# Four sample pages a run in the heads' stage, and the decay levels of the gated linear attention in two runs a head

## The chip, the cores and the metric

The kernel runs on 1 core of one Trainium2 chip. The metric is the device time of one launch in microseconds (us), as the median of three runs; the kernel before takes 1266.97 us (1264.0 to 1270.75).

## The reference, cut to what matters

One inference step of a decoder layer with two parallel head groups. 512 prompt tokens and 8 sequences of 8 sample tokens go through one input projection; eight heads do sparse attention over the 256 (128 for the prompt) best keys of an indexer, four heads do gated linear attention (GLA); both are gated and go through one output projection. The two parts that the change touches:

```python
# sample tokens: attention over 8 cache pages of 128 keys per sequence, with a mask from the indexer's top 256
s = einsum('bthd,btkhd->bthk', q, k_sel) * DH_A ** -0.5
p = softmax(where(valid, s, NEG_BIG))
out = einsum('bthk,btkhd->bthd', p, v_sel)

# GLA, inside a chunk: every pair t >= s is weighted by the decay between s and t
diff = cum[t] - cum[s]
att = einsum('bhtk,bhsk,bhtsk->bhts', qt, kt, exp(where(causal, diff, -inf)))
o = o_inter + einsum('bhts,bhsv->bhtv', att, vt)
S_new = exp(last) * S + einsum('bhsk,bhsv->bhkv', kt * exp(last - cum), vt)
```

## The kernel before

All of the 576 tokens stand as columns, in two fp32r halves (xh, xl). The projection is cut into 65 blocks of 128 output columns; `gemm` does a block in two halves, each with one weight piece (`wload`: w_raw by DMA on SP's queue, w_hi on ACT, w_lo on DVE or POOL, three buffers of each) and 48 matmuls of 288 columns (L218). These matmuls are what TensorE does most of the time. Stages follow each other: the indexer's blocks, the sample tokens' index scores (`sample_scores`, over cache pages), eight attention heads, four GLA heads, gates, output projection.

Work on the sample tokens is cut into pieces by generators and put between the weight pieces: `gemm` calls `fill` after each half, and a rate (R0, R1, RF) says how many pieces a half brings. `unit(un, w, hg)` is the attention of four sequences (w) and four heads (hg). For each half of the keys it takes the four sequences' pages (kt, 1 MB for each, as four 256 KB DMAs with page numbers read on SP), and the same over eight pages of values (vt). Its matmuls have 32 stationary columns, and four of them, for four heads, stand at the four column groups of the array (`tile_position=(0, 32 * g)`). They come in runs of two pages: `run` issues the first matmul where it is ready and holds the others right behind it, so that a run is 8 matmuls without a gemm matmul between. Two page buffers (`tag="kv", bufs=2`) serve a run. Two units run in the heads' stage (heads 4 to 7), two in the GLA stage.

In a GLA head, the decay between two tokens is built by levels B = 64, 32, 16, 8, 4, 2, 1 and the diagonal (B = 0). For each level POOL makes differences of the cumulated log decay (L879, L880), ACT the exponential (L881), DVE the products with k and q (L882, L883) into a buffer `lv_d` (two of them). Then TensorE multiplies 32 by 32 blocks into the PSUM tile `pl`: the two coarse levels in one run, every other level in a run of its own, in the order column group outside, token block i inside (L250 is a run's first matmul, L253 the others). A coarse level is copied to `att` by ACT, the others are copied under a mask `lm` to `attD` by DVE (L907, L909).

TensorE executes an fp32 matmul as two passes, so each stands twice in the trace. The order of all instructions is set by a scheduler that simulates the program; each engine, and SP's queue of DMA issues, then goes through its list in order. `page_dma` holds a page's load behind the third page before it. PSUM has three banks that rotate (`mm1`, tag "pm") and one of its own for the units (tag "pu").

Of the kernel before, what the change touches and what calls it, by code (L numbers as in the profile page):

```python
# [70 lines left out]
def shape_constants():  # L71
# [37 lines left out]
    )  # L109
    s_, t_ = i[:, None] % 32, i[None, :32]  # L110
    lm = []
    for b in LEVELS[2:]:
        lm.append((s_ // (2 * b) == t_ // (2 * b)) & (s_ % (2 * b) < b) & (t_ % (2 * b) >= b))
    lm.append(s_ == t_)
    lm = np.stack(lm, 1).astype(np.float32)
    return {k: np.ascontiguousarray(v, dtype=np.float32) for k, v in parts.items()}, lm


def build(tc, I, O):
# [3 lines left out]
    WOFF = 400  # L123
    R0, R1, RF = 0.7, 0.8, 2

# [165 lines left out]
    po_.tensor_copy(selw, sel32)  # L291
    lm = cp.tile([P, 6, 32], U8, name="lm")
    lm32 = p0.tile([P, 6, 32], F32, name="lm32")
    sy.dma_start(lm32, I["k_lm"])
# [398 lines left out]

    def unit(un, w, hg):
        qz = ev.tile([P, 4, 4, 32], F32, name="qz", tag="e0", bufs=2)
# [49 lines left out]
        pO = pm.tile([P, 512], F32, name="pOs", tag="pu", bufs=1)  # L745
        for j0 in range(0, NPAGE, 2):
            mms = []
            for j in (j0, j0 + 1):
                vt = un.tile([P, 4, 512], F32, name="vt", tag="kv", bufs=2)
                page_dma(  # L750
                    lambda bb: vt[:, bb, :], lambda r: I["cv"][r, :, 512 * hg : 512 * hg + 512].rearrange("o s c -> (o s) c"),
                    NB * NPAGE + 4 * (NPAGE * w + j), 4,
                )
                mms[:0] = [
                    partial(
                        pe.matmul, pO[32 * g : 32 * g + 32].rearrange("p (b d) -> p b d", b=4), prT[:, j, 32 * g : 32 * g + 32],
                        vt[:, :, P * g : P * (g + 1)], start=(j == 1), stop=False, tile_position=(0, 32 * g),
                    )
                    for g in range(4)
                ]  # L760
            if j0 == NPAGE - 2:
                mms += [
# [48 lines left out]

    us = chain(unit(un, 0, 1), unit(un, 1, 1))
    filler[:] = [us, R1, 0.0]
# [8 lines left out]

    wg = gl.tile([P, TP], F32, name="wg", tag="lv_d", bufs=2)
    sy.dma_start(wg[64:], I["w_gate_up"])
    wgh = gl.tile([P, TP], F32R, name="wgh", tag="lv_d", bufs=2)
    se.copy(wgh[64:], wg[64:])
# [13 lines left out]
    def log_decay(h):  # L840
        e_ = gl.tile([P, T], F32, name="ld_e", tag="lv_d", bufs=2)
        mn = gl.tile([P, T], F32, name="ld_m", tag="lv_d", bufs=2)
        for j in range(2):
# [13 lines left out]
    for h in range(HB):  # L857
# [12 lines left out]
        po_.memset(attD, 0.0)  # L870
        coarse = []
        for lv, B in enumerate(LEVELS + (0,)):
            n = T if B <= 4 else TP
            if B:
                d = gl.tile([P, T], F32, name="lv_d", tag="lv_d", bufs=2)
                half = lambda x: x[:, :n].rearrange("p (m two b) -> p m two b", two=2, b=B)
# [6 lines left out]
                ve.tensor_tensor(out=dv[:, :, 1, :], in0=dv[:, :, 1, :], in1=half(qT)[:, :, 1, :], op=ALU.mult)  # L883
                kd, qd = d, d
            else:
                kd, qd = kT, qT
            pl = mm1("pl")
            if B >= 32:
                coarse[:0] = [
                    partial(  # L890
                        pe.matmul, pl[r0 + u : r0 + u + 32, B * i : B * i + B], kd[:, P * i + r0 + u : P * i + r0 + u + 32],
                        qd[:, P * i + r0 + B : P * i + r0 + 2 * B], start=True, stop=True, tile_position=(0, r0 + u),
                    )
                    for i in range(4) for r0 in range(0, P, 2 * B) for u in range(0, B, 32)
                ]
                if B == 32:
                    run(*coarse)
                    for pl_, b_ in ((pl64, 64), (pl, 32)):
                        for r0 in range(0, P, 2 * b_):
                            se.copy(att[r0 : r0 + b_, :, r0 + b_ : r0 + 2 * b_], pl_[r0 : r0 + b_, : 4 * b_].rearrange("p (i t) -> p i t", i=4))  # L900
# [7 lines left out]
            if n == T:  # L908
                ve.copy_predicated(attD[:TS, 4, :], lm[:TS, lv - 2, :], pl[:TS, P : P + 32])  # L909
        for g in range(4):  # L910
# [14 lines left out]
        ve.tensor_mul(qE, qT, eC)  # L925
        kD = gl.tile([P, T], F32, name="kD", tag="lv_d", bufs=2)
        po_.tensor_tensor(out=kD[:, :TP].rearrange("p (i t) -> p i t", t=P), in0=cP[:, :, P - 1 : P].to_broadcast([P, 4, P]), in1=cP, op=ALU.subtract)
# [309 lines left out]
```

## Time and profile before

| | us |
|---|---|
| median of 3 runs | 1266.97 |
| lowest and highest | 1264.0, 1270.75 |
| the profiled execution | 1268.29 |
| its span on the core | 1266.5 |
| TensorE busy (98% of the span) | 1244.3 |
| DVE, ACT, POOL busy | 645.7, 540.0, 248.1 |

The profile comes from one execution. Its engines' busy times are unions of instructions in flight, so that a busy TensorE can still lose time where one kind of matmul gives way to another; the timeline, with the start of each group of matmuls, shows that. The granted TensorE clock is 0.996 of 2.4 GHz over the span. The index scores of the sample tokens lie at 145 to 212 us, heads 4 to 7 with the first two units at 382 to 648 us, and the GLA heads at 648 to 980 us.

### The profile page before, as it was taken

Reading aid. Unit: us, or ns where it says so; the run is one execution under the profiler, and the core shown is the slowest. Engines: PE = TensorE matmul, PEld = TensorE weight load, DVE = VectorE, ACT = ScalarE, POOL = GpSimd, SP = SyncE. Lnnn points to the kernel's source line nnn. Section 1 sums busy time; section 2 is a strip of 40 time slices with the busy share of each in tenths; the row PEclk is TensorE's granted clock in tenths of the full one; section 3 lists DMA queues with packets and bytes.
Section 4 is the critical chain, followed back from the end, with each engine's and each line's share of the span. In section 5 each row is a group of like instructions: output and inputs, shape, how many; then the busy total and the mean of one; then the engine's idle time right before and its main releaser. Section 6 shows DMA issues by size and latency. Waiting matters only on the chain.

```text
span 1266.5 us, 24037 instructions
## 1 busy us (share of the span) xinstructions
PE 1244.3 (98%) x9419; PEld 1133.1 (89%) x9419; DVE 645.7 (51%) x1204; ACT 540.0 (43%) x917; POOL 248.1 (20%) x307
## 2 busy tenths in 40 slices
PE   9999999999999999999999999999999999999997
PEld 8999988999998988888988888888999998888896
DVE  6677999999544334342444444444544533323233
ACT  6966775243333423242343633545444432222233
POOL 0224433343501010000104113022120210102021
PEclk9999999999999999999999999999999999999998
DMA  9642132223426566657457585574513634333335
GB/s 322 230 142 84 59 104 84 91 66 105 156 93 230 196 226 209 231 203 229 153 179 250 169 274 198 188 247 155 157 52 121 208 103 133 102 102 121 89 104 166
DMA packets 94852, 200.39 MB, mean 158 GB/s; under 512 B 11394, under 2 KB 28051, under 8 KB 94035
## 3 DMA queue, kind: packets, MB, share of 16 engines
q1 hardware_dynamic: 93650, 197.41, 47.6%
q8 instruction: 74, 1.21, 0.4%
q10 hardware_dynamic: 1088, 1.45, 0.4%
q14 instruction: 40, 0.32, 0.1%
HBM read 179.93 MB, written 18.76 MB: 157 GB/s over the span
## 4 chain that ended last, share of the span: by engine, by line
PE 80%; DVE 7%; DMA 6%; SPq 3%; ACT 2%; issue 2%; DVEq 0%; ACTq 0%
PE ps_g L218 46%; PE ps_g L226 5%; PE acc L1102 4%; PE acc L1104 4%; PE acc L1103 4%; SPq L156 2%; DVE wk L494 2%; DMA kt<-in_ck 2%; PE pOs L253 1%; PE pl L253 1%; PE pS L250 1%; PE pOs L250 1%; DMA xr<-in_xT 1%; DMA vt<-in_cv 1%; PE pS L253 1%
## 5 line engine op out<-in xcount | busy, mean ns | idle before, releaser
L218 PE MATMUL ps_g<-xh,w_hi 128*128 128x288 f32 x1824 | 402.8, 299 | 0.0
L218 PE MATMUL ps_g<-xl,w_hi 128*128 128x288 f32 x1824 | 401.7, 298 | 0.0
L218 PE MATMUL ps_g<-xh,w_lo 128*128 128x288 f32 x1824 | 398.7, 297 | 0.0
L180 ACT CAST w_hi<-w_raw 128x1024 fp32r<-128x1024 f32 x158 | 165.7, 1049 | 379.3 <-PE ps_g L218 209.2
L218 PEld LDWEIGHTS ps_g<-xh,w_hi 128*128 128x128 f32 x1824 | 296.5, 189 | 12.1 <-issue 9.2
L218 PEld LDWEIGHTS ps_g<-xh,w_lo 128*128 128x128 f32 x1824 | 296.1, 189 | 7.8 <-issue 6.3
L218 PEld LDWEIGHTS ps_g<-xl,w_hi 128*128 128x128 f32 x1824 | 296.3, 189 | 5.4 <-issue 3.7
L182 DVE TENSOR_TENSOR w_lo<-w_raw,w_hi 128x1024 fp32r<-128x1024 f32 x126 | 155.8, 1237 | 239.6 <-ACT w_hi L180 224.9
L1102 PE MATMUL acc<-w_hi,mh 128*128 128x512 f32 (+1 forms) x320 | 110.7, 347 | 0.1
L1104 PE MATMUL acc<-w_hi,ml 128*128 128x512 f32 (+1 forms) x320 | 110.8, 346 | 0.0
L1103 PE MATMUL acc<-w_lo,mh 128*128 128x512 f32 (+1 forms) x320 | 110.8, 346 | 0.0
L182 POOL TENSOR_TENSOR w_lo<-w_raw,w_hi 128x1024 fp32r<-128x1024 f32 x32 | 78.4, 2450 | 76.0 <-ACT w_hi L180 67.3
L1102 PEld LDWEIGHTS acc<-w_hi,mh 128*128 128x128 f32 x320 | 60.5, 189 | 7.8 <-DVE y L1119 0.3
L1103 PEld LDWEIGHTS acc<-w_lo,mh 128*128 128x128 f32 x320 | 60.5, 189 | 7.5
L1104 PEld LDWEIGHTS acc<-w_hi,ml 128*128 128x128 f32 x320 | 60.5, 189 | 7.5
L1122 POOL TENSOR_TENSOR y<-y,nfb 128x512 f32<-128x512 f32 (+3 forms) x25 | 28.7, 1158 | 188.5 <-ACT yjk L1121 188.5
L879 POOL TENSOR_TENSOR lv_d<-cum 128x256 f32<-128x256 f32 (+1 forms) x28 | 22.2, 794 | 181.4 <-PE pl L253 93.0
L226 PE MATMUL ps_g<-xh,w_hi 128*128 128x448 f32 x128 | 47.3, 370 | 1.1 <-ACT raw L267 1.1
L569 POOL TENSOR_TENSOR ev_sw<-ev_sw,c_s 128x576 f32<-128x576 f32 x16 | 24.7, 1542 | 120.9 <-ACT ev_sw L566 120.9
L226 PE MATMUL ps_g<-xh,w_lo 128*128 128x448 f32 x128 | 47.1, 368 | 0.0
L226 PE MATMUL ps_g<-xl,w_hi 128*128 128x448 f32 x128 | 47.0, 367 | 0.0
L419 DVE SCALAR_TENSOR_TENSOR sc<-rl,wtok,sc 128x256 f32<-128x256 f32 (+2 forms) x45 | 34.5, 800 | 10.4 <-ACT rl L414 10.1
(336 smaller groups left out, 1680.8 us busy)
## 6 DMA issues: line engine op xcount, KB each, us to landing
w_raw<-in_w SPq DMA_DIRECT2D x126, 512.0 KB, 3.7
kt<-in_ck SPq DMA_DIRECT2D x128, 256.0 KB, 5.1
vt<-in_cv SPq DMA_DIRECT2D x128, 256.0 KB, 4.8
w_raw<-in_wo SPq DMA_DIRECT2D x32, 512.0 KB, 3.7
xr<-in_xT SPq DMA_DIRECT2D x16, 288.0 KB, 4.5
xt<-in_xp SPq DMA_DIRECT2D x4, 1024.0 KB, 5.7
st<-in_state SPq DMA_DIRECT2D x8, 512.0 KB, 4.6
out_ss<-st SPq DMA_DIRECT2D x8, 512.0 KB, 4.0
```

Of the source, the lines that this page charges most:

```text
L156: d = sy.dma_start(dst(j), src(bass.ds(v[j], 1)))
L180: se.copy(hi, raw)
L182: lo_eng[0].tensor_tensor(out=lo, in0=raw, in1=hi.bitcast(F32), op=ALU.subtract)
L218: pe.matmul(ps[:, j, :HT], wt, xt[:, j * HT : (j + 1) * HT], start=(k == 0 and n == 0), stop=(k == NK - 1 and n == 2),)
L226: pe.matmul(ps[:, 0, :TQ], wt[:, c], xt[:, P:T], start=(k == 0 and n == 0), stop=(k == NK - 1 and n == 2))
L250: lead = first()
L253: f()
L419: ve.scalar_tensor_tensor(out=sc[i], in0=rl[:, :n], scalar=wcol, in1=sc[i], op0=ALU.mult, op1=ALU.add)
L1102: pe.matmul(acc, mh[k][:, tsl], wh, start=(k == 0), stop=False)
L1103: pe.matmul(acc, mh[k][:, tsl], wl, start=False, stop=False)
L1104: pe.matmul(acc, ml[k][:, tsl], wh, start=False, stop=(k == NK - 1))
L1122: po_.tensor_tensor(out=yc, in0=yc, in1=nfb[:r, cs], op=ALU.mult)
```

## The change

1. `unit` gets a `span`: the pages in a run, with `span + 1` page buffers. The two units of the heads' stage take 4 (runs of 16 matmuls, five buffers, rate R0 0.42 in place of 0.7, since a unit now has 6 pieces and not 10); the two of the GLA stage take 2 (as before, with three buffers). The pool of page buffers is closed between the stages and opened again.
2. The decay levels are taken in the order 64, 32, 0, 16 and 8, 4, 2, 1, and each four are one run into one PSUM tile, the last level first. Levels 16 to 1 take as moving columns only the second halves of their blocks, 16 of 32. Token block i is now outside and column group g inside, and the two coarse levels put odd blocks at the other column groups. Copies follow after the run, from 16 columns each; the mask is laid out for that. `lv_d` gets five buffers.
3. The accumulator of the sample tokens' index scores (`pacc`) moves from the three rotating PSUM banks to the units' own bank.
4. The scratch of dynamic DMAs is set to 1024.

```diff
@@ -121,7 +122,7 @@
     ve, se, pe, po_, sy = nc.vector, nc.scalar, nc.tensor, nc.gpsimd, nc.sync
     NPOOL = I["ck"].shape[0]
     WOFF = 400
-    R0, R1, RF = 0.7, 0.8, 2
+    R0, R1, RF = 0.42, 0.8, 2
...
@@ -431,7 +432,7 @@
 
     def sample_scores():
         lq = [qiS[:, b].rearrange("p h t -> p (h t)") for b in range(NB)]
-        acc = mm1("pacc")
+        acc = pm.tile([P, 512], F32, name="pacc", tag="pu", bufs=1)
         rls = []
...
-    def unit(un, w, hg):
+    def unit(un, w, hg, span):
...
-            for b0 in (0, 2):
+            for b0 in range(0, 4, span):
                 mms = []
-                for bb in (b0, b0 + 1):
-                    kt = un.tile([P, 4, 512], F32, name="kt", tag="kv", bufs=2)
+                for bb in range(b0, b0 + span):
+                    kt = un.tile([P, 4, 512], F32, name="kt", tag="kv", bufs=span + 1)
...
                     mms[:0] = [
-                        partial(pe.matmul, S[32 * g : 32 * g + 32], qz[:, g, bb, :], kv[:, :, g, :], start=False, stop=(bb == 2), tile_position=(0, 32 * g))
+                        partial(pe.matmul, S[32 * g : 32 * g + 32], qz[:, g, bb, :], kv[:, :, g, :], start=False, stop=(bb == 4 - span), tile_position=(0, 32 * g))
                         for g in range(4)
                     ]
                 run(*mms)
...
-        for j0 in range(0, NPAGE, 2):
+        for j0 in range(0, NPAGE, span):
             mms = []
-            for j in (j0, j0 + 1):
-                vt = un.tile([P, 4, 512], F32, name="vt", tag="kv", bufs=2)
+            for j in range(j0, j0 + span):
+                vt = un.tile([P, 4, 512], F32, name="vt", tag="kv", bufs=span + 1)
...
-            if j0 == NPAGE - 2:
+            if j0 == NPAGE - span:
...
-    us = chain(unit(un, 0, 0), unit(un, 1, 0))
+    us = chain(unit(un, 0, 0, 4), unit(un, 1, 0, 4))
     filler[:] = [us, R0, 0.0]
...
+    un_s.close()
+    un, un_s = pool("unit2", 1, side="right")
+    us = chain(unit(un, 0, 1, 2), unit(un, 1, 1, 2))
     filler[:] = [us, R1, 0.0]
...
-        coarse = []
-        for lv, B in enumerate(LEVELS + (0,)):
-            n = T if B <= 4 else TP
+
+        mms, outs = [], []
+        off = 0
+        for B in (64, 32, 0, 16, 8, 4, 2, 1):
+            n = TP if B > 4 else T
+            if B in (64, 8):
+                pl, off = mm1("pl"), 0
             if B:
-                d = gl.tile([P, T], F32, name="lv_d", tag="lv_d", bufs=2)
+                d = gl.tile([P, T], F32, name="lv_d", tag="lv_d", bufs=5)
                 half = lambda x: x[:, :n].rearrange("p (m two b) -> p m two b", two=2, b=B)
...
-                kd, qd = d, d
-            else:
-                kd, qd = kT, qT
-            pl = mm1("pl")
+            level = []
+            mms.append(level)
             if B >= 32:
-                coarse[:0] = [
-                    partial(
-                        pe.matmul, pl[r0 + u : r0 + u + 32, B * i : B * i + B], kd[:, P * i + r0 + u : P * i + r0 + u + 32],
-                        qd[:, P * i + r0 + B : P * i + r0 + 2 * B], start=True, stop=True, tile_position=(0, r0 + u),
-                    )
-                    for i in range(4) for r0 in range(0, P, 2 * B) for u in range(0, B, 32)
-                ]
-                if B == 32:
...
-                pl64 = pl
+
+                for i in range(4):
+                    for r0 in range(0, P, 2 * B):
+                        for u in range(0, B, 32):
+                            ro = r0 + u + B * (i % 2)
+                            c0 = off + B * (i // 2)
+                            s0 = P * i + r0
+                            level.append(partial(
+                                pe.matmul, pl[ro : ro + 32, c0 : c0 + B], d[:, s0 + u : s0 + u + 32], d[:, s0 + B : s0 + 2 * B],
+                                start=True, stop=True, tile_position=(0, ro),
+                            ))
+                for r0 in range(0, P, 2 * B):
+                    for odd in range(2):
+                        outs.append(partial(
+                            se.copy, att[r0 : r0 + B].rearrange("p (j two) t -> p j two t", two=2)[:, :, odd, r0 + B : r0 + 2 * B],
+                            pl[r0 + B * odd : r0 + B * odd + B, off : off + 2 * B].rearrange("p (j t) -> p j t", j=2),
+                        ))
+                off += 2 * B
                 continue
...
-            run(*(
-                partial(pe.matmul, pl[32 * g : 32 * g + 32, 32 * i : 32 * i + 32], kd[:, c], qd[:, c], start=True, stop=True, tile_position=(0, 32 * g))
-                for g in range(4) for i in range(4 if n == TP or g > 1 else 5) for c in (slice(P * i + 32 * g, P * i + 32 * g + 32),)
-            ))
-            ve.copy_predicated(attD[:, :4, :], lm[:, lv - 2, :].unsqueeze(1).to_broadcast([P, 4, 32]), pl[:, :P].rearrange("p (i t) -> p i t", i=4))
...
+            w = 16 if B else 32
+            for i in range(4 if n == TP else 5):
+                for g in range(4 if i < 4 else 2):
+                    c = slice(P * i + 32 * g, P * i + 32 * g + 32)
+                    mv = d[:, c].rearrange("p (m two b) -> p m two b", two=2, b=B)[:, :, 1, :] if B else qT[:, c]
+                    o = pl[32 * g : 32 * g + 32, off + w * i : off + w * i + w]
+                    level.append(partial(
+                        pe.matmul, o.rearrange("p (m b) -> p m b", b=B) if B else o, (d if B else kT)[:, c], mv,
+                        start=True, stop=True, tile_position=(0, 32 * g),
+                    ))
...
+            off += w * (4 if n == TP else 5)
+            if B in (16, 1):
+                run(*(m for level in reversed(mms) for m in level))
+                for f in outs:
+                    f()
+                mms, outs = [], []
...
+    nc = bacc.Bacc("TRN2", target_bir_lowering=False, num_devices=1, dynamic_dma_scratch_size=1024)
```

On TensorE's list in the heads' stage, before, the first half's keys are two runs of 8 matmuls with other work between (kt is a page, qz the masked queries, pS the scores):

```order
1620 L250 MATMUL pS_4572<-kt_4588,qz_4564 32x512
1621 L253 MATMUL pS_4572<-kt_4588,qz_4564 32x512 x3
1622 L253 MATMUL pS_4572<-kt_4574,qz_4564 32x512 x4
...
1663 L250 MATMUL pS_4572<-kt_4691,qz_4564 32x512
1664 L253 MATMUL pS_4572<-kt_4691,qz_4564 32x512 x3
```

In the changed kernel the same place is one run:

```order
1638 L251 MATMUL pS_4639<-kt_4683,qz_4631 32x512
1639 L254 MATMUL pS_4639<-kt_4683,qz_4631 32x512 x3
1640 L254 MATMUL pS_4639<-kt_4669,qz_4631 32x512 x4
1641 L254 MATMUL pS_4639<-kt_4655,qz_4631 32x512 x4
1642 L254 MATMUL pS_4639<-kt_4641,qz_4631 32x512 x4
```

Four pages now stand together and the stretch of gemm matmuls between the two pairs is gone; 96 gemm matmuls stand before the next such run. On TensorE's list for the last GLA head, before, levels 16 and 8 and, later, levels 4 and 2 stand between gemm matmuls (pl is the PSUM tile, lv_d a level's products):

```order
3562 L250 MATMUL pl_10948<-lv_d_10942 32x32
3563 L253 MATMUL pl_10948<-lv_d_10942 32x32 x15
3564 L250 MATMUL pl_10972<-lv_d_10966 32x32
3565 L253 MATMUL pl_10972<-lv_d_10966 32x32 x15
...
3590 L250 MATMUL pl_10996<-lv_d_10990 32x32
3591 L253 MATMUL pl_10996<-lv_d_10990 32x32 x17
3592 L250 MATMUL pl_11023<-lv_d_11017 32x32
3593 L253 MATMUL pl_11023<-lv_d_11017 32x32 x17
```

In the changed kernel the same head's eight levels are two runs:

```order
3509 L251 MATMUL pl_10904<-lv_d_10917 32x16
3510 L254 MATMUL pl_10904<-lv_d_10917 32x16 x15
3511 L254 MATMUL pl_10904<-qT_10789,kT_10900 32x32 x18
3512 L254 MATMUL pl_10904<-lv_d_10911 32x32 x8
3513 L254 MATMUL pl_10904<-lv_d_10905 32x64 x8
...
3538 L251 MATMUL pl_10982<-lv_d_11001 32x16
3539 L254 MATMUL pl_10982<-lv_d_11001 32x16 x17
3540 L254 MATMUL pl_10982<-lv_d_10995 32x16 x18
3541 L254 MATMUL pl_10982<-lv_d_10989 32x16 x18
3542 L254 MATMUL pl_10982<-lv_d_10983 32x16 x16
```

The number of matmuls is the same, 120 a head; 50 stand in the first run and 70 in the second. Over the whole program the stretches of 32-column matmuls between others fall from 57 to 44: by 8 in the heads' stage (18 to 10) and by 5 in the GLA stage (34 to 29). ACT copies 24 coarse pieces and not 12; the instruction counts of the other engines and of SP's queue stay.

## Rows read from the trace of the kernel before

**Rows 1.** The page: engines' busy time and span share; the last chain by engine.

```profile
PE 1244.3 (98%) x9419; PEld 1133.1 (89%) x9419; DVE 645.7 (51%) x1204; ACT 540.0 (43%) x917; POOL 248.1 (20%) x307
...
PE 80%; DVE 7%; DMA 6%; SPq 3%; ACT 2%; issue 2%; DVEq 0%; ACTq 0%
```

**Rows 2.** Waits of TensorE: who for whom, us in total, times, longest.

```profile
PE pq L463 <- ACT rl L466: 3.3, 3, 1.7
PE pS L250 <- DMA kt<-in_ck: 2.2, 3, 1.0
PE pOs L250 <- DMA vt<-in_cv: 1.9, 2, 1.3
```

**Rows 3.** TensorE's timeline, a run of two pages: start us, us, what, xcount.

```profile
393.89 0.43 PE L218 MATMUL ps_g<-xh,w_lo 128*128 128x288 f32 x2
...
394.43 0.43 PE L218 MATMUL ps_g<-xh,w_hi 128*128 128x288 f32 x2
394.79 0.62 PE L250 MATMUL pS<-kt,qz 128*32 128x512 f32 x1
...
396.64 0.53 PE L218 MATMUL ps_g<-xh,w_lo 128*128 128x288 f32 x2
397.01 0.42 PE L218 MATMUL ps_g<-xl,w_hi 128*128 128x288 f32 x2
```

**Rows 4.** TensorE's timeline, a run of two pages with four matmuls more.

```profile
600.98 0.43 PE L218 MATMUL ps_g<-xl,w_hi 128*128 128x288 f32 x2
...
603.08 1.04 PE L253 MATMUL pOs<-vaS,prT 128*32 128x512 f32 x8
...
604.42 0.42 PE L218 MATMUL ps_g<-xh,w_lo 128*128 128x288 f32 x2
```

**Rows 5.** TensorE's timeline around the coarse levels, 752 us.

```profile
751.95 0.42 PE L218 MATMUL ps_g<-xl,w_hi 128*128 128x288 f32 x2
...
753.49 0.42 PE L218 MATMUL ps_g<-xh,w_lo 128*128 128x288 f32 x2
```

**Rows 6.** TensorE's timeline around levels 16 and 8, 679 us.

```profile
678.82 0.42 PE L218 MATMUL ps_g<-xl,w_hi 128*128 128x288 f32 x2
...
680.98 0.43 PE L218 MATMUL ps_g<-xh,w_lo 128*128 128x288 f32 x2
```

**Rows 7.** TensorE's timeline around levels 4 and 2, 853 us.

```profile
852.60 0.30 PE L218 MATMUL ps_g<-xh,w_hi 128*128 128x288 f32 x1
...
854.52 0.40 PE L218 MATMUL ps_g<-xh,w_hi 128*128 128x288 f32 x1
854.75 0.43 PE L218 MATMUL ps_g<-xh,w_lo 128*128 128x288 f32 x2
```

**Rows 8.** TensorE's timeline, eight matmuls of 8 columns (16 passes) over column groups.

```profile
210.95 0.20 PE L250 MATMUL pacc<-rl,wall 128*32 128x8 f32 x1 [0.24 <-DVE rl L477]
...
211.00 0.18 PE L250 MATMUL pacc<-rl,wall 128*32 128x8 f32 x1
211.01 0.25 PE L253 MATMUL pacc<-rl,wall 128*32 128x8 f32 x11
```

**Rows 9.** All engines' timeline, from a level run to the next, last head.

```profile
920.74 0.80 POOL L879 TENSOR_TENSOR lv_d<-cum 128x288 f32<-128x288 f32 x1 [2.11 <-PE pl L253]
...
925.52 0.45 DVE L883 TENSOR_TENSOR lv_d<-lv_d,qT 128x288 f32<-128x288 f32 x1
927.58 0.14 PEld L250 LDWEIGHTS pl<-lv_d 128*32 128x32 f32 x2 [0.16 <-issue]
```

**Rows 10.** SP's timeline: the eight DMA issues of two pages.

```profile
395.92 4.32 SPq L156 DMA_DIRECT2D kt<-in_ck  x8
```

**Rows 11.** The tile kt: its DMAs from issue to landing.

```profile
DMA to landing us min/median/max: 2.6/5.1/7.7
```

**Rows 12.** Waits of ACT: for a free buffer of w_hi.

```profile
ACT w_hi L180 <- PE ps_g L218: 209.2, 66, 7.7
```

**Rows 13.** Index scores: stretch, length, busy us of PE, PEld, DVE, ACT, POOL (count), clock.

```profile
145.00:212.00 67.00, 62.96 (x450) 55.64 (x449) 62.86 (x135) 50.18 (x80) 24.94 (x14) 1.00 0.32 101
```

More of the change, by code (lines that the diff above doesn't have):

```diff
@@ L109, in shape_constants @@
     )
-    s_, t_ = i[:, None] % 32, i[None, :32]
+    s_, j_ = i[:, None] % 32, np.arange(16)[None, :]
     lm = []
     for b in LEVELS[2:]:
-        lm.append((s_ // (2 * b) == t_ // (2 * b)) & (s_ % (2 * b) < b) & (t_ % (2 * b) >= b))
-    lm.append(s_ == t_)
-    lm = np.stack(lm, 1).astype(np.float32)
+        t_ = j_ // b * 2 * b + b + j_ % b
+        lm += [(s_ // (2 * b) == t_ // (2 * b)) & (s_ % (2 * b) < b)] * 4
+    lm += [s_ == np.arange(32)[None, :]] * 4
+    lm = np.concatenate(lm, 1).astype(np.float32)
     return {k: np.ascontiguousarray(v, dtype=np.float32) for k, v in parts.items()}, lm
@@ L291, in build @@
     po_.tensor_copy(selw, sel32)
-    lm = cp.tile([P, 6, 32], U8, name="lm")
-    lm32 = p0.tile([P, 6, 32], F32, name="lm32")
+    lm = cp.tile([P, 448], U8, name="lm")
+    lm32 = p0.tile([P, 448], F32, name="lm32")
     sy.dma_start(lm32, I["k_lm"])
@@ L756, in unit @@
                         pe.matmul, pO[32 * g : 32 * g + 32].rearrange("p (b d) -> p b d", b=4), prT[:, j, 32 * g : 32 * g + 32],
-                        vt[:, :, P * g : P * (g + 1)], start=(j == 1), stop=False, tile_position=(0, 32 * g),
+                        vt[:, :, P * g : P * (g + 1)], start=(j == span - 1), stop=False, tile_position=(0, 32 * g),
                     )
@@ L809, in build @@
     pd_s.close()
-    us = chain(unit(un, 0, 1), unit(un, 1, 1))
+    un_s.close()
+    un, un_s = pool("unit2", 1, side="right")
+    us = chain(unit(un, 0, 1, 2), unit(un, 1, 1, 2))
     filler[:] = [us, R1, 0.0]
@@ L821, in build @@
     G = 1.0 / 16.0
-    wg = gl.tile([P, TP], F32, name="wg", tag="lv_d", bufs=2)
+    wg = gl.tile([P, TP], F32, name="wg", tag="lv_d", bufs=5)
     sy.dma_start(wg[64:], I["w_gate_up"])
-    wgh = gl.tile([P, TP], F32R, name="wgh", tag="lv_d", bufs=2)
+    wgh = gl.tile([P, TP], F32R, name="wgh", tag="lv_d", bufs=5)
     se.copy(wgh[64:], wg[64:])
@@ L840, in log_decay @@
     def log_decay(h):
-        e_ = gl.tile([P, T], F32, name="ld_e", tag="lv_d", bufs=2)
-        mn = gl.tile([P, T], F32, name="ld_m", tag="lv_d", bufs=2)
+        e_ = gl.tile([P, T], F32, name="ld_e", tag="lv_d", bufs=5)
+        mn = gl.tile([P, T], F32, name="ld_m", tag="lv_d", bufs=5)
         for j in range(2):
@@ L883, in build @@
                 ve.tensor_tensor(out=dv[:, :, 1, :], in0=dv[:, :, 1, :], in1=half(qT)[:, :, 1, :], op=ALU.mult)
-                kd, qd = d, d
-            else:
-                kd, qd = kT, qT
-            pl = mm1("pl")
+            level = []
+            mms.append(level)
             if B >= 32:
-                coarse[:0] = [
-                    partial(
-                        pe.matmul, pl[r0 + u : r0 + u + 32, B * i : B * i + B], kd[:, P * i + r0 + u : P * i + r0 + u + 32],
-                        qd[:, P * i + r0 + B : P * i + r0 + 2 * B], start=True, stop=True, tile_position=(0, r0 + u),
-                    )
-                    for i in range(4) for r0 in range(0, P, 2 * B) for u in range(0, B, 32)
-                ]
-                if B == 32:
[L897 to L900, printed above, removed]
-                pl64 = pl
-                continue
@@ new lines, in build @@
+            m0 = 64 * (3 - (B - 1).bit_length() + 1) if B else 320
+            for to, src, mk in (
+                (attD[:, :4], pl[:, off : off + 4 * w], lm[:, m0 : m0 + 4 * w]),
+                (attD[:TS, 4:5], pl[:TS, off + 4 * w : off + 5 * w], lm[:TS, m0 : m0 + w]),
+            )[: 1 if n == TP else 2]:
+                if B:
+                    v = lambda x: x.rearrange("p (m b) -> p m b", b=B)
+                    outs.append(partial(ve.copy_predicated, to.rearrange("p i (m two b) -> p (i m) two b", two=2, b=B)[:, :, 1, :], v(mk), v(src)))
+                else:
+                    v = lambda x: x.rearrange("p (i t) -> p i t", t=32)
+                    outs.append(partial(ve.copy_predicated, to, v(mk), v(src)))
@@ L925, in build @@
         ve.tensor_mul(qE, qT, eC)
-        kD = gl.tile([P, T], F32, name="kD", tag="lv_d", bufs=2)
+        kD = gl.tile([P, T], F32, name="kD", tag="lv_d", bufs=5)
         po_.tensor_tensor(out=kD[:, :TP].rearrange("p (i t) -> p i t", t=P), in0=cP[:, :, P - 1 : P].to_broadcast([P, 4, P]), in1=cP, op=ALU.subtract)
```

3 lines of the change are left out of this document (removed).

## The prediction, made before the change was run

> **What bounds the kernel now.** First the page: TensorE is busy 98% of the span and holds 80% of the chain that ended last; DVE has 7% of it, DMAs 6% [rows 1]. So the time is TensorE's list, plus where TensorE stands still. Second, its waits: the largest are 3.3 us for ACT to empty a PSUM bank of index scores and 2.2 and 1.9 us for pages of keys and values [rows 2]. Together they are 7.4 us of 1266.5, so little is to be had from waiting; the rest must come from what TensorE executes. Third, the timeline, because a busy share doesn't show what a change of matmul kind costs. The reader is to take the distance between two gemm groups on either side of a run, less the gemm matmuls within it.
>
> A pair of gemm matmuls takes 0.27 us (393.89 to 394.43 holds two) [rows 3]. From 394.43 to 397.01 are 2.58 us; less two pairs, a run of two pages costs 2.04 us [rows 3]. A run with four matmuls more costs 604.42 - 600.98 - 0.54 = 2.90 us [rows 4]. Four matmuls at four column groups are two passes, so two rounds cost 0.86, one round of 512 columns 0.43. The run of 8 matmuls is four rounds, 1.72 us; the other 0.32 us is paid once a stretch, going in and coming out (the first gemm pair after it takes 0.37 in place of 0.27).
>
> The decay levels, read the same way and with the 0.32 taken off: the 16 coarse matmuls cost 1.54 - 0.54 - 0.32 = 0.68 us [rows 5]; levels 16 and 8, 32 matmuls, 2.16 - 0.54 - 0.32 = 1.30 [rows 6]; levels 4 and 2, 36 matmuls, 2.15 - 0.27 - 0.32 = 1.56 [rows 7]; level 1 and the diagonal are 36 matmuls again, and I take 1.56 for them. That is 5.10 us a head, 20.4 us for four heads. A level matmul thus costs some 43 ns and a pass 20 to 22 ns, though it moves only 32 columns, for which a round at the pages' pace (0.43 us / 512) would be 27 ns for four of them. In the list before, four or five neighbours use the same column group. A place where neighbours use four different groups is the short run of index scores: its first pass starts at 210.95, the first of the second round at 211.00, and its last one, 0.18 us long, ends at 211.26, so starts at 211.08 [rows 8]. Rounds two to four, the whole of 12 passes, start within 0.08 us, after some 0.05 for the first: about 0.032 us a round of four passes, 8 ns a pass.
>
> **The change, part by part.**
>
> Stretches. Page runs of the heads' stage go from 16 to 8, and stretches of 32-column matmuls fall by 13 in all. The page matmuls themselves stay, at 0.43 a round. 13 x 0.32 = 4.2 us less. Nothing lies beside that: it is TensorE's own time.
>
> Level matmuls. As many as before, 120 a head, but neighbours now stand at different column groups. I price a round at 0.032 us or at its columns times 0.84 ns, whichever is more. The first run: level 16 is 8 rounds, the diagonal 10 (two of them half empty), level 32 four, all at 0.032, and level 64 four rounds of 64 columns at 0.054: 0.92 us. The second: 8 + 3 x 10 rounds at 0.032: 1.22 us. Together 2.14 a head; 5.10 - 2.14 = 2.96, in four heads 11.8 us less. The half width adds nothing to this, since 16 columns at 0.84 ns are 13 ns and the round's floor of 0.032 decides. What isn't shown is the pace of matmuls whose moving columns lie in steps (every second column at level 1). The bounds: if a pass keeps its 21 ns, 0 us; if it even paid double for the step, a 16-column pass is a 32-column pass again, still 0; if a round of 16 columns went at its 13 ns, 38 + 8 rounds would save another 0.019 each, 3.5 us over four heads. I take 11.8, by the nearest row [rows 8].
>
> A rule of the Trainium skill speaks against this: TensorE: Matmul & The Clock Gate, section Wait — 56ns, not 53.3ns?, says that matmuls start at least about 25 ns apart however few columns they move. By that rule 240 passes a head are an estimated 6.0 us, 3.6 us more than now over four heads, and only the stretches would gain. The level runs of before, at 20 to 22 ns a pass, are already below that figure, and the short run at 8 ns is far below [rows 6, 8].
>
> What the levels wait for. The second run needs levels 2 and 1, whose buffers are free only when the first run has read levels 64 and 32. In the trace the way from a level run to the next two levels' data is: POOL starts at 920.74, DVE's last product ends at 925.97, 5.2 us [rows 9]. In the new list at least 47 gemm matmuls, 6.3 us, stand between a head's two runs. So nothing is late, with 1.1 us to spare at the tightest; without that cover each head pays what it lacks, 1 to 2 us where DVE or POOL has other work in the way. ACT's 12 copies more and DVE's masked copies lie beside the gemm.
>
> Pages. A run of four now needs three or four new pages, 3 MB with one held in the fifth buffer. Two pages' eight issues take SP 4.32 us [rows 10], so three take 6.5; the last lands after a median 5.1, at most 7.7 us [rows 11]: 11.6 to 14.2 us after the run before. The nearest two runs have 96 gemm matmuls between them, 12.8 us; the others 15 to 22. So one or two waits of up to 1.4 us, against 4.1 us of page waits now [rows 2], and the GLA stage has a third buffer for its runs of two. I take the waits as unchanged; bounds -4.1 (all gone) and +4. Behind a page load that waits for its buffer stand the weight loads on SP's queue. They have cover: ACT waits for a free w_hi buffer 66 times, 3.2 us in the mean [rows 12], with two further pieces, two times 6.5 us of gemm, split ahead.
>
> The PSUM bank. With the accumulator elsewhere all three rotating banks serve the index scores, so the 3.3 us [rows 2] may go. But DVE is busy 62.9 of 67 us there [rows 13] with the top-k rounds whose mask the next heads need, so what TensorE gains it may wait for later. Between 0 and 3.3 I take half, 1.6 us.
>
> The dynamic scratch and the mask's layout move no instruction of TensorE; 0.
>
> Sum: 4.2 + 11.8 + 1.6 = 17.6 us. From the profiled execution's 1268.29 that gives 1250.7; the median is 1.3 lower, so 1249.4 us.
>
> **The rivals.**
>
> The interleaving brings nothing: small matmuls go one by one at 21 ns whatever their column group. Then only stretches and bank are left, 5.8 us: 1261. For it, that in the trace every level run goes at that pace [rows 6, 7]; against it, rows 8. By the Trainium skill's rule named above it would be an estimated 1265.
>
> Something eats part of the gain: levels late by 1 to 2 us a head and page waits of 1 to 2 us in half of the eight long runs, some 8 to 10 us: 1258.
>
> Slower: SP's queue. In the heads' stage up to five page loads can stand in one piece, 20 issues, 10.8 us by rows 10, with no weight load among them, and 3 to 5 MB are then in flight ahead of it. If that makes a weight piece later than its cover of some 16 us, TensorE stops for every one of the eight long runs; it decides from about 2.2 us a run (17.6 / 8). With 3 us wasted at weights and 2 at the pages a run, 40 us: 1290. Against it: the bytes and the rate are the same over the stage, and the five waits for pages now hold 4.1 us together [rows 2].
>
> **How the numbers follow.** Forecast 0.70, part eaten 0.13, no interleaving 0.12, slower 0.05. A difference under 0.5%, 6.3 us, can't be told from none here: 1260.6 is the line. The forecast's own range is 1242 (round at its columns, page waits gone) to 1256; the range goes to 1260 for the partly eaten case. Faster: 0.70 + 0.13 + 0.02 of the third case, 0.85; same 0.10; slower 0.05.
>
> **What would show it.** In the profile after: level runs in two stretches a head of 1.24 and 1.54 us with entry (right), or of about 2.4 and 3.3 (wrong: no interleaving); page runs of 3.8 us; waits of pS and pOs for DMAs near 4 us (wrong if over 10), none of gemm matmuls for w_hi or w_lo; no wait of pl for lv_d; pq's 3.3 us gone, and whether a wait on DVE stands at 214 to 265 us in its place. The prediction is wrong if the GLA stage isn't shorter by some 12 us.

## The result, and the profile after

The changed kernel takes **1257.64 us** (median of 6 runs, 1257.15 to 1259.17) against 1266.18 us (6 runs); the ratio is 0.9926, 95% interval 0.9911 to 0.9940. It is faster, by 8.5 us, about half of the 17.6 us that were forecast. The profiled executions are 1268.29 and 1257.15 us, 11.1 apart.

The page after: busy time by engine, share of the span and instructions.

```profile
PE 1228.7 (98%) x9419; PEld 1120.7 (89%) x9419; DVE 648.1 (52%) x1204; ACT 542.3 (43%) x930; POOL 253.7 (20%) x307
```

TensorE is busy 15.6 us less than in [rows 1], on as many instructions, and the span is 11.1 us shorter: it stands still more than it did. The list of what it waits for (who for whom, us in total, times, longest) says where:

```profile
PE pOs L251 <- DMA vt<-in_cv: 2.9, 2, 1.9
PE pS L251 <- DMA kt<-in_ck: 2.7, 1, 2.7
PE pt L648 <- DVE p L637: 1.7, 1, 1.7
PE pacc L251 <- ACT rl L467: 1.5, 1, 1.5
...
PE pl L251 <- ACT lv_d L888: 1.1, 1, 1.1
...
PE pt L963 <- POOL kD L960: 0.9, 1, 0.9
PE pl L251 <- ACT kD L959: 0.8, 1, 0.8
```

The 3.3 us of pq [rows 2] are gone, with 1.5 and 1.7 us in their place. Three new rows are of level runs (pl) and of kD's transposes (pt) behind them. All 5.6 us of page waits (pOs and pS) stand in the GLA stage; of the 4.1 us before [rows 2], some 2.7 stood there already and 1.3 in the heads' stage.

**The runs themselves.** A run of four pages with four matmuls more, in TensorE's timeline (start us, us, what, count):

```profile
588.30 0.43 PE L219 MATMUL ps_g<-xl,w_hi 128*128 128x288 f32 x2
...
592.12 1.04 PE L254 MATMUL pOs<-vaS,prT 128*32 128x512 f32 x8
...
593.46 0.42 PE L219 MATMUL ps_g<-xh,w_lo 128*128 128x288 f32 x2
```

Read as in [rows 4]: 5.16 us less two gemm pairs (0.54) is 4.62, which is ten rounds of 0.43 and one entry of 0.32. A first level run, and a second one (of the next head) with kD's five transposes behind it:

```profile
750.16 0.43 PE L219 MATMUL ps_g<-xh,w_lo 128*128 128x288 f32 x2
...
752.00 0.42 PE L219 MATMUL ps_g<-xh,w_hi 128*128 128x288 f32 x2
...
843.62 0.42 PE L219 MATMUL ps_g<-xh,w_lo 128*128 128x288 f32 x2
...
845.30 0.66 PE L963 MATMUL pt<-c_ident,kD 128*128 128x128 f32 x4
...
845.82 0.51 PE L219 MATMUL ps_g<-xl,w_hi 128*128 128x288 f32 x2
846.17 0.42 PE L219 MATMUL ps_g<-xh,w_hi 128*128 128x288 f32 x2
```

The first is 1.84 - 0.54 = 1.30 us. The second is 2.55 - 0.54, less 0.52 for the transposes (845.30 to 845.82): 1.49. Together 2.79 where 1.24 + 1.54 were forecast. A pass costs 8.4 ns in the second ((1.49 - 0.32) / 140), against 20 to 22 before [rows 6, 7].

**The stages.** The GLA stage is taken from the first bias matmul of its pages to the last head's 16 state matmuls. Before:

```profile
648.31 0.39 PE L707 MATMUL pS<-biasS,selw 128*128 128x512 bf16 x1
...
962.66 1.07 PE L1003 MATMUL pO<-st,Qb 128*32 128x256 f32 x16
```

After:

```profile
643.76 0.39 PE L708 MATMUL pS<-biasS,selw 128*128 128x512 bf16 x1
...
951.77 1.07 PE L1033 MATMUL pO<-st,Qb 128*32 128x256 f32 x16
```

All that comes before the GLA stage gained 4.55 us. The GLA stage went from 314.35 to 308.01 us and gained 6.3; level runs and five stretches fewer are worth 11.8 + 1.6 = 13.4. So some 7 us of TensorE's gain are lost inside this stage.

**A late page run**, at 676.77 us. All engines' timeline, cut to what it hangs on:

```profile
665.50 1.46 PE L254 MATMUL pS<-kt,qz 128*32 128x512 f32 x11
...
666.12 2.16 DVE L889 TENSOR_TENSOR lv_d<-lv_d,kT 128x256 f32<-128x256 f32 x3
...
668.20 1.21 DVE L183 TENSOR_TENSOR w_lo<-w_raw,w_hi 128x1024 fp32r<-128x1024 f32 x1
...
669.44 0.34 SPq L178 DMA_DIRECT2D w_raw<-in_w  x1
...
670.45 2.45 SPq L157 DMA_DIRECT2D kt<-in_ck  x4
...
676.77 0.59 PE L251 MATMUL pS<-kt,qz 128*32 128x512 f32 x1 [2.73 <-DMA kt<-in_ck]
```

The run before it has read its pages at 666.96. The page's four DMAs are issued from 670.45: SP's queue holds a weight load ahead of them, which waits for DVE to have split the piece in its buffer (w_lo, to 669.41), and DVE did three level products first. The page is late by 2.7 us, less than the 3.5 us that it stood behind the weights. Two further runs, at 840.05 and 849.02 us, wait for pages of values, 1.0 and 1.9 us; by the distance of the gemm matmuls around them the three are 2.8, 1.1 and 3.4 us too long, 7.3 us in all. In the heads' stage no run waits for a page any more.

**The clock behind a wait.** The run at 849.02 us is 3.4 us too long and waits only 1.9. TensorE's timeline there, and then a stretch of TensorE alone (stretch, length, busy us and count, granted clock, DMA share, GB/s):

```profile
849.02 0.69 PE L251 MATMUL pOs<-vt,prT 128*32 128x512 f32 x1 [1.90 <-DMA vt<-in_cv]
...
849.57 2.79 PE L254 MATMUL pOs<-vt,prT 128*32 128x512 f32 x11
```

```profile
849.40:852.80 3.40, 3.40 (x18) 0.50 0.49 164
```

Eleven passes take 2.79 us here and 1.46 us in the run at 665.50. From 849.4 to 852.8 us the granted clock is 0.50 (1.2 GHz); in the rest of this GLA stage, and in the whole of it before, it is 1.00 (2.4 GHz). 3.4 us at half the clock are 1.7 us lost, part of them in gemm matmuls behind the run, and no list of waits shows them. Not every wait has such a fall behind it: the 2.73 us at 676.77 have none.

**A late level run**, last head, in all engines' timeline:

```profile
908.11 0.54 PE L254 MATMUL pl<-lv_d 128*32 128x32 f32 x31
...
909.74 0.78 POOL L952 COPY eL<-ev_ec 128x4 f32<-128x4 f32 x1 [29.11 <-ACT ev_ec L950]
...
910.79 0.67 POOL L886 TENSOR_TENSOR lv_d<-cum 128x288 f32<-128x288 f32 x1
...
915.26 0.45 DVE L890 TENSOR_TENSOR lv_d<-lv_d,qT 128x288 f32<-128x288 f32 x1
...
915.81 2.29 POOL L960 TENSOR_TENSOR kD<-kT,kD 128x576 f32<-128x576 f32 x1 [0.79 <-ACT kD L959]
915.85 0.18 PE L251 MATMUL pl<-lv_d 128*32 128x16 f32 x1 [0.76 <-ACT kD L959]
...
918.15 0.66 PE L963 MATMUL pt<-c_ident,kD 128*128 128x128 f32 x4 [0.91 <-POOL kD L960]
```

The first run ends at 908.65 and frees the buffers of levels 2 and 1. POOL takes them up at 910.79, 2.1 us later, after three small copies of which the first had to wait for ACT; DVE's last product ends at 915.71. That is 7.1 us from run to data, and 47 gemm matmuls (6.3 us) stand between. (The row of the second run names ACT's kD, which ended within 0.02 us of that product; the matmuls read the product.) Then kD, which uses the same buffers and comes last on POOL, makes the transposes wait again.

### The profile page after: what moved, and what is told of

It reads as the page before. It is cut to its first block, busy times and chain, and to the rows that moved or that the text cites. A ratio compares the mean times of both kernels' runs of the same rounds, so it can differ in the third digit from the quotient of the medians.

```text
span 1255.4 us, 23889 instructions
## 1 busy us (share of the span) xinstructions
PE 1228.7 (98%) x9419; PEld 1120.7 (89%) x9419; DVE 648.1 (52%) x1204; ACT 542.3 (43%) x930; POOL 253.7 (20%) x307
## 4 chain that ended last, share of the span: by engine, by line
PE 84%; DVE 8%; DMA 2%; ACT 2%; issue 2%; POOL 1%; SPq 1%; DVEq 0%; ACTq 0%
PE ps_g L219 48%; PE ps_g L227 6%; PE acc L1132 5%; PE acc L1134 5%; PE acc L1133 5%; DVE wk L495 2%; PE pOs L254 2%; DVE m L492 1%; PE pS L254 1%; PE acc L1137 1%; PE acc L1136 1%; PE pOs L251 1%; DVE kcl L461 1%; DMA vt<-in_cv 1%; PE pS L251 1%
## 5 line engine op out<-in xcount | busy, mean ns | idle before, releaser
L219 PEld LDWEIGHTS ps_g<-xh,w_hi 128*128 128x128 f32 x1824 | 296.6, 189 | 13.9 <-issue 10.7
```

What stands on the lines that cost most here:

```text
L219: pe.matmul(ps[:, j, :HT], wt, xt[:, j * HT : (j + 1) * HT], start=(k == 0 and n == 0), stop=(k == NK - 1 and n == 2),)
```

## The experiments

Each is set against the changed kernel (1257.6 us, ratio 0.9926); "the GLA stage" is measured as above.

**Only the levels' part.**

```diff
-    R0, R1, RF = 0.42, 0.8, 2
+    R0, R1, RF = 0.7, 0.8, 2
...
-        acc = pm.tile([P, 512], F32, name="pacc", tag="pu", bufs=1)
+        acc = mm1("pacc")
...
-                    kt = un.tile([P, 4, 512], F32, name="kt", tag="kv", bufs=span + 1)
+                    kt = un.tile([P, 4, 512], F32, name="kt", tag="kv", bufs=span)
...
-    us = chain(unit(un, 0, 0, 4), unit(un, 1, 0, 4))
+    us = chain(unit(un, 0, 0, 2), unit(un, 1, 0, 2))
...
```

(and likewise for the buffers of vt; the pool of page buffers stays open between the stages)

> The kernel before with the levels' part alone: interleaved level runs, five level buffers, the new mask. Sample pages stay at two a run with two buffers at the old rate 0.7, and the score accumulator stays in the rotating banks. Theory A (the levels' list really is some 11 us shorter, and waits in the GLA stage take back about half of it, whatever the heads' stage does): the GLA stage gains 5 to 8 us, in all 1258 to 1262, ratio 0.994 to 0.997; waits of pS, pOs and pl in the GLA stage of 6 to 10 us in place of about 3. Rival C (the GLA stage loses its gain through the new page buffers and the shifted start of its pages, so through the pages' part): without that part the whole 11 to 13 us appear, 1253 to 1255, ratio 0.990 to 0.9915.

Measured: 1264.79 us, ratio 0.9977 (0.9962 to 0.9992). The GLA stage is 310.9 us, 3.5 shorter than before. Its largest waits there:

```profile
PE pl L254 <- issue: 3.1, 2, 2.0
PE pS L251 <- DMA kt<-in_ck: 2.8, 2, 2.6
PE pOs L251 <- DMA vt<-in_cv: 1.7, 3, 0.7
```

The loss is there without the pages' part, so rival C falls; it is larger than theory A expected, 9.9 us of 13.4, and the time lies outside both ranges. All its waits in the stage are 10.0 us where they were 3.5 before, and the granted clock is 0.50 from 690.3 to 693.7 and from 772.2 to 775.6 us: 6.5 and 3.4 us. The largest row is of waits inside level runs for which the profile names nothing ("issue"); what they are stays open.

**Only the pages' part and the bank**: the kernel before with runs of four pages in the heads' stage, three page buffers in the GLA stage, the accumulator's bank and the changed scratch.

> The kernel before with the pages' part and the accumulator's own bank, the levels as before. Theory A: the heads' stage gains eight stretches of 0.32 us and the 1.4 us that one page wait took, about 4 us; the bank gains nothing, since DVE's top-k rounds set the end of that stage; the GLA stage as before or up to 1 us shorter by its third page buffer: 1261 to 1263, ratio 0.996 to 0.9975. Rival: the bank's 1.6 us do come through, 1260, ratio 0.995. Rival C (GLA loses by the pages' part): the GLA stage is 3 to 5 us longer than before, in all 1265 to 1267, ratio 0.999 to 1.0005.

Measured: 1264.58 us, ratio 0.9980 (0.9969 to 0.9992), between the ranges of theory A and rival C, and by parts in neither: what lies before the GLA stage gained 8.3 us (bias matmul at 640.01), more than expected, and the GLA stage lost 2.4 (316.8). For the same work it lost 4.1, since this order puts 13 gemm matmuls (1.7 us) of the stage behind its end. What was gained beyond the 4 us comes from the index scores. The last transpose of ev_v behind them, in the kernel before, in the changed one and in this one, with the same 1630 of TensorE's 9419 records ahead of it in each:

```profile
265.13 0.42 PE L605 MATMUL pt<-c_ident,ev_v 128*128 128x128 f32 x1
264.14 0.42 PE L606 MATMUL pt<-c_ident,ev_v 128*128 128x128 f32 x1
260.09 0.33 PE L605 MATMUL pt<-c_ident,ev_v 128*128 128x128 f32 x1
```

Here the 3.3 us of pq come through and more, 5.0 us; in the changed kernel, where TensorE waits 1.7 us for DVE's p at 247.92 and 1.1 us for DVE at 262.04, 1.0 us is left. This kernel's order has neither wait. One wait in the GLA stage is as large as what that stage lost:

```profile
PE pl L250 <- DVE lv_d L885: 4.5, 1, 4.5
```

It is the last head's last level run, which this kernel's order puts 0.6 us of gemm behind the one before it (that ends at 925.66), while its data need 5.0 us (to 930.65); from 930.6 to 934.0 us the granted clock is 0.50. No instruction of the levels was changed here. So the waits of this stage depend on where the order happens to put the runs, and a single gain of 4 us in it must be read with that in mind. The levels' part alone gains 2.4 us and this part alone 2.6, and both together 8.5: the parts don't add up.

**The order of the columns undone.**

```diff
-            for i in range(4 if n == TP else 5):
-                for g in range(4 if i < 4 else 2):
+            for g in range(4):
+                for i in range(4 if n == TP or g > 1 else 5):
```

(and likewise for the coarse levels)

> The changed kernel with one thing undone: within a level, neighbouring matmuls use the same column group again (four or five in a row), all matmuls, stretches, columns and buffers as in the changed kernel. If the column group of the neighbour sets the pace, a pass costs 21 ns again in place of 8: the two level stretches of a head take about 2.3 and 3.1 us in place of 1.3 and 1.6, 2.5 us a head, 10 us in all; of that the waits of the GLA stage give back part, since pages and levels then come in time: 1262 to 1267, ratio to before 0.997 to 1.001. If the order is worth nothing and the gain came from the half width or from the fewer stretches, the runs stay at 1.3 and 1.6 us and the time at 1257 to 1258, ratio 0.993.

Measured: 1261.99 us, ratio 0.9959 (0.9940 to 0.9977). The level runs:

```profile
754.96 0.43 PE L219 MATMUL ps_g<-xh,w_lo 128*128 128x288 f32 x2
...
757.61 0.42 PE L219 MATMUL ps_g<-xh,w_hi 128*128 128x288 f32 x2
```

```profile
682.66 3.02 PE L254 MATMUL pl<-lv_d 128*32 128x16 f32 x138
```

2.65 - 0.54 = 2.11 us in place of 1.30, and the second run (its passes above; 682.09 to 686.35, read likewise) 3.20 in place of 1.49: 2.5 us a head, 10 us in all, by the neighbour's column group alone; a pass costs 18 to 21 ns again. The time rises only 4.4 us, and so does the GLA stage (312.4): TensorE's waits in it fall from 9.1 to 3.6 us in the list, and each of the two executions has one stretch of 3.4 us at a clock of 0.50. That is the mirror of what happened to the change.

**The GLA stage's pages loaded once.**

```diff
+                    kt = held[len(mms) // 4] if hg and held else un.tile([P, 4, 512], F32, name="kt", tag="kv", bufs=span + 1)
...
+                vt = held[len(mms) // 4] if hg else un.tile([P, 4, 512], F32, name="vt", tag="kv", bufs=span + 1)
```

> The changed kernel with the loads of the GLA stage's sample pages left out after the first two: all sixteen page runs of that stage read these two pages (this leaves out the rest of the pages, so the sample attention of four heads is computed from the wrong pages), matmuls and places as in the changed kernel. Theory A: no run waits for a page, the 7.3 us of the three late runs (at 673.75, 838.72 and 846.83 us) come back, less what then waits for levels: 1250 to 1252, ratio 0.987 to 0.989. Rival D (the pages only cover what the levels would wait for anyway, so the wait moves to pl and pt): 1255 to 1257, ratio 0.991 to 0.993, with 3 to 5 us more of waits of pl and pt.

Measured: 1252.35 us, ratio 0.9892 (0.9868 to 0.9915): 0.35 us above theory A's range, 2.7 below rival D's. The GLA stage is 303.2 us, 4.8 shorter than in the changed kernel. Part of the wait did move, as rival D has it; what is left there are the levels, and a clock of 0.50 from 669.9 to 673.3 us:

```profile
PE pl L251 <- DVE lv_d L894: 3.9, 2, 2.2
```

**Two page buffers in the GLA stage** (`bufs=2` there in place of 3).

> The changed kernel with two page buffers in the GLA stage, as before, in place of three; all else as changed. If the third buffer is what kept the page waits of that stage from being worse (its place is then why the levels' part alone gained so little), page waits there grow by 2 to 5 us: 1259.5 to 1262, ratio 0.994 to 0.996. If the third buffer is worth nothing, since the loads start late for another reason (SP held up at the weights), 1257 to 1258, ratio 0.9925.

Measured: 1258.72 us, ratio 0.9932 (0.9911 to 0.9952); the GLA stage is 309.2 us. The medians put a third buffer at 1 us, between the two cases; these runs can tell that neither from nothing nor from 3 us.

**The accumulator back in the rotating banks** (`acc = mm1("pacc")`).

> The changed kernel with the score accumulator back in the three rotating banks. The prediction gave its own bank half of 3.3 us. If the gain is given back to DVE's top-k rounds, as the waits of pt for p (1.7 us) and of pacc for ACT (1.5 us) in the changed kernel suggest: within 0.7 us of the changed kernel, 1257 to 1258.5. If the half is real, 1259 to 1260; if all of it is, 1260.5 to 1261. The wait of pq for rl, some 3.3 us, is back in every case.

Measured: 1259.94 us, ratio 0.9938 (0.9918 to 0.9958). The interval holds all three cases, and its profiled execution spans 3,876 us, so that its waits can't be read beside the others; inconclusive.

**Page runs further apart** (`R1` 0.5 in place of 0.8).

> The changed kernel with the rate of the GLA stage's page runs at 0.5 in place of 0.8: most runs are then 96 gemm matmuls apart (12.8 us) where four of the changed kernel's were 22 to 34 apart; the last three of the sixteen come 24 to 38 matmuls apart at the end of the stage. Theory A (page runs that follow one another faster than pages come): of the 7.3 us of page waits 2 to 4 us stay, in the last runs: 1253 to 1255.5, ratio 0.989 to 0.991. Rival D (the wait moves to pl and pt, or the end of the stage takes all back): 1257 to 1259, ratio 0.9925 to 0.994.

Measured: 1267.59 us, ratio 1.0000 (0.9985 to 1.0015), 10 us slower than the changed kernel. The waits from 640 to 970 us:

```profile
PE pl L251 <- DVE lv_d L890: 7.7, 3, 3.5
PE pOs L251 <- DMA vt<-in_cv: 1.7, 1, 1.7
```

Pages are nearly on time, as theory A has it, but rival D decides, and beyond its range: page runs had been TensorE's work while the levels were made ready. Taken away from there, they leave level runs waiting 3.2 us at 670.49 and 3.5 at 901.73, and the last output transposes, moved to the end of the stage, wait 3.6 us for ACT until 970.38. Behind each of these three waits the granted clock is 0.50 for 3.4 us (from 671.4, 903.5 and 971.7 us), 5.1 us in all where the changed kernel loses 1.7. The other executions bear it out: the mean granted clock of the twelve is 0.988 to 0.996, and the one at 0.996 is the fastest, 1262.97 us.

**Six level buffers** (`bufs=6` for lv_d).

> The changed kernel with six level buffers in place of five. If the levels are late because a buffer is free only when the run before has read it, the 4 us of waits of pl and pt go to about 1: 1254 to 1255.5, ratio 0.990 to 0.991. If they are late because the chain through POOL, ACT and DVE takes longer than the gemm matmuls ahead of the run (33 to 47), a sixth buffer changes only where they stand: 1257 to 1258.5, ratio 0.9925 to 0.9935. I expect the second.

Measured: 1258.62 us, ratio 0.9931 (0.9910 to 0.9952). As the second theory has it, no gain; pl waits 4.8 us for DVE in its profiled execution, which took 1262.05 us. Free buffers aren't what the levels lack.

**kD ahead of the levels.**

```diff
+        kD = gl.tile([P, T], F32, name="kD", tag="kD")
...
+        po_.tensor_tensor(out=kD, in0=kT, in1=kD, op=ALU.mult)
+
         attD = gl.tile([P, 5, 32], F32, name="attD")
...
-        kD = gl.tile([P, T], F32, name="kD", tag="lv_d", bufs=5)
```

> The changed kernel with kD (the keys decayed to the chunk's end) in a buffer of its own and its POOL, ACT and POOL steps ahead of the levels, in place of behind levels 2 and 1 in their buffers. Theory A (in the GLA stage POOL's chain after the first level run, two levels and then kD, is longer than the gemm matmuls ahead of the second run and its transposes): the waits of pl and pt for kD at 759.92 and 914.79 us, 0.9 and 1.8 us, go, and the second level run is 2 to 3 us less late: 1254 to 1256, ratio 0.990 to 0.992. Rival E (what sets the time is where the order places page and level runs against one another, and any edit shifts the waits about): 1257 to 1260, the same sum of waits at other places.

Measured: 1257.51 us, ratio 0.9926 (0.9907 to 0.9944). The waits for kD are gone, and others came:

```profile
PE pOs L251 <- DMA vt<-in_cv: 2.3, 2, 1.2
PE pl L251 <- ACT lv_d L894: 2.1, 1, 2.1
PE pt L776 <- ACT ob L773: 1.7, 1, 1.7
PE pS L251 <- DMA kt<-in_ck: 1.3, 1, 1.3
```

By itself this gains nothing: rival E. The same kernel was executed and profiled once more (the label names a rate that this kernel doesn't have):

> A second look at the same kernel, for where its waits stand in another execution: the same places within 0.5 us.

1259.0 us. Not so: in the last head the transposes of ob ahead of the first level run were 1.7 us late in the one execution (908.28 us), and the second level run 1.7 us late in the other (918.44). A page run at 763 us took 0.4 us more, and one at 678 us 2.7 more, of which 1.3 are wait and the rest a clock of 0.50 from 677.8 us. Waits of this size move by 1 to 2 us between executions of one program.

**kD early, and page runs a little further apart** (`R1` 0.75): runs of two pages stand at least 48 gemm matmuls (6.4 us) apart, where some were 22 to 38 apart in the changed kernel.

> The kernel of the run before (kD early, in its own buffer) with the rate of the GLA stage's page runs at 0.75 in place of 0.8, by which no two page runs stand closer than 44 gemm matmuls, where they were down to 21 to 30. Theory A (page runs that follow one another faster than pages come; with the levels' own chain shorter, cover for them is no longer missing): page waits of the GLA stage 1 to 4 us, 1252 to 1255.5, ratio 0.988 to 0.991. Rival E (any edit of the order only shifts the waits about): 1256.5 to 1260, ratio 0.9915 to 0.9945.

Measured: **1252.32 us, ratio 0.9884 (0.9861 to 0.9908)**, faster than both kernels. The largest waits from 640 to 970 us, and the stage's two ends:

```profile
PE pl L251 <- ACT lv_d L894: 2.1, 1, 2.1
PE pl L251 <- ACT w_hi L181: 1.1, 1, 1.1
```

```profile
645.62 0.39 PE L708 MATMUL pS<-biasS,selw 128*128 128x512 bf16 x1
...
947.61 1.07 PE L1034 MATMUL pO<-st,Qb 128*32 128x256 f32 x16
```

No page is waited for in the stage, and the granted clock is 1.00 in all of it; 302.0 us, 12.4 shorter than before: nearly the 13.4 that TensorE's list was said to lose. With kD early already there, the rate brings 5.2 us. The rate of 0.75 without the early kD wasn't run, so whether it needs kD stays open.

**kD early and the pages loaded once.**

> kD early, and the GLA stage's page loads left out after the first two (the page runs read these two again, which leaves the other pages out of four heads' sample attention). If pages and the levels' chain are the two causes and there is no third, the stage comes to within 2 us of what TensorE needs, some 13 us less than before: 1248.5 to 1250.5, ratio 0.985 to 0.987. If the levels are late for another reason (the first run of a head waits for ACT's exponentials and DVE's products), 3 to 4 us of waits of pl stay: 1251 to 1253, ratio 0.988 to 0.989.

Measured: 1251.79 us, ratio 0.9880 (0.9859 to 0.9902), the second case: what waits is the first level run of the first head, for ACT (the granted clock is 1.00 in the whole stage):

```profile
PE pl L251 <- ACT lv_d L898: 2.8, 1, 2.8
```

The GLA stage is 300.4 us. The kernel with all its pages (1252.32) is as fast as this one within what can be told: of the page waits nothing is left to be had.

## Why the prediction was right and wrong

- **Stretches, 0.32 us each**: right; four pages and four matmuls cost 4.62 us, as its prices have it. With the page wait of 1.3 us that went as well, the heads' pages gave about 3.9 us.
- **Level matmuls, 11.8 us**: right, 2.79 us a head with entry where 2.78 were forecast. Undoing the order alone brings 10 us of level runs back; the other 1.8 stay, and no run separates what they come from. The rival that small matmuls go one by one falls: the second run takes 8.4 ns a pass. The Trainium skill (TensorE: Matmul & The Clock Gate, section Wait — 56ns, not 53.3ns?) has starts at least some 25 ns apart; the 8.4 ns of this trace differ, and the measurement decides.
- **"I take the waits as unchanged"**: this step failed. Page waits went from 4.1 to 5.6 us in the list, inside the bound of +4, but their place moved: 1.3 us left the heads' stage, and in the GLA stage, in runs of two pages, 2.7 became 5.6. I had priced the long runs of the heads' stage with care and passed over the GLA stage with its third buffer, which the run with two couldn't tell from nothing. Loading the pages once gives 4.8 us of the stage back.
- **"Nothing is late" at the levels**: failed, by 2.8 us in the list. The 5.2 us of [rows 9] hold where POOL stands ready: the row shows it idle for 2.11 us until the run had read the buffer. In the new list POOL has three copies ahead, one of them behind ACT, and starts 2.1 us after the run ends; from run to data it is 7.1 us, against the 6.3 of cover. That made a second run 0.8 us late. The other 2.0 weren't in the sum at all: 1.1 for the first run of the first head, 0.9 for kD, in the same buffers and last on POOL.
- **The clock** was no term of the sum: 1.7 us, behind the wait at 849.02 us.
- **The bank, half of 3.3 us**: between nothing and all. 1.0 us is left in the changed kernel, as DVE's waits come in its place, and 5.0 us came with the pages' part alone; the run made for it couldn't tell.

So the step that decided is the waits of the GLA stage, taken as unchanged while TensorE's list there became 13.4 us shorter. That the waits and the clock are all of what was lost can be worked out for each kernel whose GLA stage has the shorter list in the same places: 13.4, less what its list of waits from 640 to 970 us has above the 3.5 us of before, less 1.7 us for each stretch of 3.4 us at a clock of 0.50.

| kernel | waits, us | clock falls | gain worked out, us | gain of the stage, us |
|---|---|---|---|---|
| the changed kernel | 9.1 | 1 | 6.1 | 6.3 |
| only the levels' part | 10.0 | 2 | 3.5 | 3.5 |
| pages loaded once | 4.5 | 1 | 10.7 | 11.1 |
| two page buffers | 9.9 | 1 | 5.3 | 5.2 |
| kD early, rate 0.75 | 4.5 | 0 | 12.4 | 12.4 |
| kD early, pages once | 3.3 | 0 | 13.6 | 14.0 |

(Left out are the rate of 0.5, which moves work out of the stage, six level buffers, where waits lie inside the stretches at 0.50, and kD early by itself, whose traces lack the matmul at the stage's start.)

By place: ahead of the GLA stage 4.2 us were forecast (eight stretches and the bank) and 4.55 came; in it 13.4 and 6.3; behind it 0.2. That is the 11.1 us between the profiled executions. The medians are 8.5 apart: the profiled execution of before was 2.1 us above its median, that of after 0.5 below.

By its own mark (wrong if the GLA stage isn't some 12 us shorter) the forecast was wrong in place, and what happened is the second rival, "something eats part of the gain", 1258 us, to which I gave 0.13; only its page waits stood in another stage. That the time lies in the stated range is owed to this rival, since the forecast's own range ended at 1256. The rest of the gain was real: a small shift of two orders brought 5.3 us of it back.

## What to carry to other kernels

Where TensorE's list is made shorter in a stage that it fills to 98%, price every supply in that stage again, since the cover of each has become shorter by what was saved; measure a supply from the event that frees its buffer, and add what its first engine still has ahead of it in its order. Fill-in work (here page runs) is cover for other waits too: spreading it evenly may cost more than it saves, and the two must be moved together. Beside the list of waits read the granted clock behind each of them; here a fall added 1.7 us to a wait of 1.9. In this case half of the gain of a stage hung on the order; a prediction of such a change should leave room for that until the order has been read for the shortest distances between runs.

## What the runs showed of the hardware

Passes with 32 stationary columns whose neighbours use other column groups start 8.4 ns apart in a run of 140 (16 columns moved, at level 1 every second one), and about 20.6 ns apart when the neighbour uses the same group, all else equal: 1.17 and 2.88 us for the same 70 matmuls. Moving columns in steps cost nothing that shows, beside the 8 ns of [rows 8]. Behind some waits of TensorE in the GLA stage, of 1.9 us at 849.02 in the changed kernel and of 3.2 and 3.5 us with the rate of 0.5, the granted clock was 0.50 for 3.4 us; behind others, of 2.73 us at 676.77, it stayed at 1.00, and what decides isn't shown.
